# A pool of its own for the small buffers of a float32 decoder block: every large on-chip buffer starts 32 to 192 bytes lower

## The chip, the cores and the metric

The kernel runs on one core of one Trainium2 chip. The time is the device time of one execution in microseconds (us). It was taken three times before the change: 2767.97, 2766.76 and 2764.39 us, median 2766.76 us. A fourth execution, the one that the hardware profiler recorded, took 2759.24 us; its span, from the first to the last instruction, is 2757.5 us, so 1.7 us lie around the span. All durations below come from that execution.

## What is computed

One layer of a decoder for 512 tokens with 2048 channels, all in float32, cut here to what matters:

```python
def mixer(h, pos, w_in, w_a, w_b, w_o):
    proj = h @ w_in
    q_a, k_a, v_a, q_b, k_b, v_b, qi, ki, wi, g_a, g_b = jnp.split(proj, offsets, axis=-1)
    y_a = stick_breaking_attention(q_a, k_a, v_a) @ w_a
    y_b = dsa_attention(rope(q_b), rope(k_b), v_b, rope(qi), rope(ki), wi) @ w_b
    merged = jax.nn.sigmoid(g_a) * y_a + jax.nn.sigmoid(g_b) * y_b
    return merged @ w_o

def conv_ffn(h, w_up, conv_w, conv_b, w_down):
    u = h @ w_up
    u = conv_b + sum(conv_w[i] * shifted(u, i) for i in range(3))
    a, b = jnp.split(u, 2, axis=-1)
    return (jax.nn.silu(a) * b) @ w_down
```

Around both parts stand an RMS norm with a scale and a shift that are computed from a vector c (a 2048 x 12288 matrix times c), and a gated residual add. The products with the large weight matrices are nearly all of the work.

## The kernel before

**Products of three.** Each large product of float32 numbers is made of three matmuls of the type float32r. Every operand is split in two: a high part (a copy to float32r on ScalarE, line 133 for weights, 162 for data) and a low part (the difference, on VectorE, lines 135 and 164). `mm3` (lines 142 to 146) then issues high x high (L143), high x low (L144) and low x high (L145) into one accumulator. Its first argument is the stationary operand of the array, its second the moving one. Weights come by DMA from SyncE's queue into eight buffers `raw` (128 partitions x 4096 bytes), and their two parts lie in three buffers `wh` and three `wl` of the same size. Data live in 62 slots `F` of 128 x 2048 bytes.

**Which operand moves.** A group of rows in the profile names it as `out<-moving,stationary`. In the first stage (the query part of the token indexer, 16 steps of 7 products) the data `F` move, 512 columns wide, past weights in `wh` and `wl`. In the next (the values of the first attention) the weights move and the data stand. Then come the 31 Strassen units of the projection (`unit`, line 199 on), where data halves of 256 columns move past weights. After the two attentions follow w_a and w_b (512 columns, data moving), eight units of w_o, the up-projection (512 wide for its first three pairs of tiles, then units of 256), and the down-projection, where weights move again, 512 wide. In the last part of that, four column blocks for each of four token blocks, both operands lie in slots `F`. The two products with `w_tail` take only 80 columns of weights at a time: step k has its weights 320 x k bytes into the buffer.

**Where buffers lie.** The order of work is the program's, arranged by a scheduler that knows no addresses. A pool lays out its buffers one tag after another, in the order in which tags are first asked for. A buffer takes a multiple of 32 bytes. All buffers were in one pool `sb`, so a small one (`eps`, 4 bytes in each partition, or `c_col`, 64 bytes) shifts all that come after it:

| buffers | first address before | remainder by 128 | remainder by 256 |
|---|---|---|---|
| `F` (62 x 2048 bytes), `raw` (8 x 4096), `T` | 26912, 153888, 22816 | 32 | 32 |
| `wl`, `wh` (3 x 4096 each) | 186720, 199008 | 96 | 96 |
| `w` (2 x 2048) | 211296 | 96 | 96 |
| `sp`, `ta` (2 x 2048 each) | 215456, 219552 | 32 | 160 |
| `soft` (5120) | 223680 | 64 | 192 |

The buffers of one tag follow each other without a gap, so all of a tag have its remainder.

Of the kernel before, what the change touches and what calls it, by code (L numbers as in the profile page):

```python
# [10 lines left out]
F32 = mybir.dt.float32  # L11
# [7 lines left out]
P = 128  # L19
D = 2048  # L20
S = 512
KT = D // P
HD = 128
NH = 8
IDXH = 16
IDXD = 64
TOPK = 128
NQB = S // P
# [48 lines left out]
def block_kernel(ctx: ExitStack, tc: tile.TileContext, A: dict, out: bass.AP):  # L77
    nc = tc.nc
    sb = ctx.enter_context(tc.tile_pool(name="sb", bufs=1))
    pp = ctx.enter_context(tc.tile_pool(name="pp", bufs=1, space=PSUM))  # L80
    dr = ctx.enter_context(tc.tile_pool(name="dr", bufs=1, space=bass.MemoryType.DRAM))

# [2 lines left out]
    def nm(s):  # L85
        counter[0] += 1
        return f"{s}_{counter[0]}"

    def t2k(tag, bufs, dt=F32, w=S):
        return sb.tile([P, w], dt, tag=tag, bufs=bufs, name=nm(tag))  # L90
# [26 lines left out]
    g_mix, g_ffn = (vec[:, 96 + i * KT : 96 + (i + 1) * KT] for i in range(2))  # L117
    mask = sb.tile([P, 2, P], BF16, tag="mask", name="mask")
    cw = sb.tile([P, 2 * NJ, 4], F32, tag="cw", name="cw")
    eps = sb.tile([P, 1], F32, tag="eps", name="eps")  # L120
    nc.vector.memset(eps, EPS)


# [200 lines left out]
        return cb  # L324

    cb = c_spread()
    c_col = sb.tile([P, KT], F32, tag="c_col", name="c_col")
    nc.scalar.dma_start(c_col, A["c_col"])
    act(c_col, c_col, AF.Silu)

# [1 line left out]
    def rms(squares, blocks=range(NQB), bank=outs):  # L332

        total = bank()
        at = slice(blocks[0] * P, (blocks[-1] + 1) * P)
        for b in blocks:
            for i, t in enumerate(squares):
                mm(total[:, b : b + 1], t[:, b * P : (b + 1) * P], ones[:, :1], start=b == blocks[0] and i == 0,
                   stop=i == len(squares) - 1, skip_group_check=True)
        r = sb.tile([P, NQB], F32, tag="r", bufs=2, name=nm("r"))  # L340
        rb = r[:, blocks[0] : blocks[-1] + 1]
        act(rb, total[:, blocks[0] : blocks[-1] + 1], AF.Sqrt, scale=1.0 / D, bias=eps)
        nc.vector.reciprocal(rb, rb)
        wide = t2k("T", 2)
        for b in blocks:
            ts(wide[:, b * P : (b + 1) * P], ident, r[:, b : b + 1], None, ALU.mult)
        yield
        out = bank()
        mm(out[:, at], ones, wide[:, at], start=True, stop=True)
        yield out  # L350
# [138 lines left out]

    def rope_tables():  # L490
        f0, f1, f2, f3, f123, f23, fr = _turn_parts()
        inv = sb.tile([64, 1], F32, tag="inv", name="inv")
        nc.scalar.dma_start(inv, A["inv_freq"])
        pos = t2k("T", 2, I32)[:64]
        nc.scalar.dma_start(pos, A["positions"].to_broadcast([64, S]))
        turn = [t2k("w", 2)[:64] for _ in range(2)]

        def nearest(o, i, step):
            m = 1.5 * 2.0**23 * step
            ts(o, i, m, m, ALU.add, ALU.subtract)  # L500

        for half in range(2):
            at = slice(half * HALF, (half + 1) * HALF)
            q1, q2 = (t[:, at] for t in turn)
            tmp = sb.tile([P, 5 * HALF], F32, tag="soft", name=nm("soft"))[:64]
            ang, a2, a1, a0, rn = (tmp[:, i * HALF : (i + 1) * HALF] for i in range(5))
            nc.vector.tensor_copy(ang, pos[:, at])
            ts(ang, ang, inv, None, ALU.mult)
            nearest(a2, ang, 2.0**20)
            tt(ang, ang, a2, ALU.subtract)  # L510
            yield
            nearest(a1, ang, 2.0**8)
            tt(ang, ang, a1, ALU.subtract)
            nearest(a0, ang, 2.0**-4)
            tt(ang, ang, a0, ALU.subtract)
            small = ang
            ts(small, ang, fr, None, ALU.mult)
            yield
            stt(small, a0, f123, small, ALU.mult, ALU.add)
            stt(small, a1, f23, small, ALU.mult, ALU.add)  # L520
            stt(small, a2, f3, small, ALU.mult, ALU.add)
            ts(q1, a1, f0, None, ALU.mult)
            stt(q1, a2, f1, q1, ALU.mult, ALU.add)
            yield
            nearest(rn, q1, 1.0)
            tt(q1, q1, rn, ALU.subtract)
            ts(q2, a1, f1, None, ALU.mult)
            stt(q2, a2, f2, q2, ALU.mult, ALU.add)
            nearest(rn, q2, 1.0)
            tt(q2, q2, rn, ALU.subtract)  # L530
            yield
            stt(q1, a0, f0, q1, ALU.mult, ALU.add)
            tt(q1, q1, q2, ALU.add)
            nearest(rn, q1, 1.0)
            tt(q1, q1, rn, ALU.subtract)
            tt(q1, q1, small, ALU.add)
            yield
            nearest(rn, q1, 1.0)
            tt(q2, q1, rn, ALU.subtract)
            ts(q1, q2, 0.25, None, ALU.add)  # L540
            nearest(rn, q1, 1.0)
            tt(q1, q1, rn, ALU.subtract)
            yield
        TWO_PI = float(np.nextafter(np.float32(2 * np.pi), np.float32(0)))
        q1, q2 = turn
        for n, step in enumerate((64, 32)):
            o = t2k("raw", 8, w=1024)
            for i in range(P // step):
                at = slice(step * i, step * i + step)
                act(o[at, :S], q1[:step], AF.Sin, scale=TWO_PI)  # L550
                act(o[at, S:], q2[:step], AF.Sin, scale=TWO_PI if i % 2 else -TWO_PI)
                if i % 2:
                    yield
            save(rope_d[n], o)
# [109 lines left out]
    for k in range(0, KT, 2):  # L664
        r = t2k("w", 2)
# [19 lines left out]
    def strips(a, b, c):  # L685

        return [b[:, 3 * P : 4 * P], c[:, : 2 * P], b[:, : 3 * P], a[:, : 4 * P]]
# [7 lines left out]
    def indexer():  # L695
# [6 lines left out]
        for b in range(NQB):  # L702
            nc.tensor.transpose(wps[:, b * IDXH : (b + 1) * IDXH], tail[IDXD:TN, b * P : (b + 1) * P],
                                ident[IDXD:TN, IDXD:TN])
        wi = sb.tile([P, NQB, IDXH], F32, tag="wi", name="wi")
        nc.vector.tensor_copy(wi.rearrange("p b h -> p (b h)"), wps[:, : NQB * IDXH])
        bias.extend(slot()[:, : (b + 1) * P] for b in range(1, NQB))
        yield
# [36 lines left out]
        for b in range(1, NQB):  # L745
            sc = bias[b]
            for i in range(TOPK // 8):
                m8 = sb.tile([P, 8], F32, tag="m8", bufs=2, name=nm("m8"))
                nc.vector.max(out=m8, in_=sc)
                nc.vector.match_replace(out=sc, in_to_replace=m8, in_values=sc, imm_value=TAKEN)  # L750
                if i % 2:
                    yield
            ts(sc, sc, TAKEN, NEG, ALU.not_equal, ALU.mult)
# [5 lines left out]

    vb = [[], []]  # L760
    index = indexer()
    run(index)
    run(index)
# [117 lines left out]
    ya = [split(o) for o in ya]  # L881

    def sparse_1(q, k):
        m = sb.tile([P, NQB], F32, tag="m", bufs=2, name=nm("m"))
        s = sb.tile([P, NQB], F32, tag="s", bufs=2, name=nm("s"))
        soft = sb.tile([P, 10 * P], F32, tag="soft", name=nm("soft"))
        lg = strips(*(acc() for _ in range(3)))
        p = strips(*of_soft(soft))
        for b in (2, 0, 1, 3):
            W = (b + 1) * P  # L890
            mm(lg[b], q[:, b * P : (b + 1) * P], k[:, :W], start=b > 0, stop=True, skip_group_check=True)
        for b in (2, 0, 1, 3):
            nc.vector.tensor_tensor_reduce(out=p[b], in0=lg[b], in1=bias[b], scale=HD**-0.5, scalar=-3.0e38,
                                           op0=ALU.add, op1=ALU.max, accum_out=m[:, b : b + 1])
        last = ts(m, m, -1.0, None, ALU.mult)
        for b in (2, 0, 1, 3):
            act(p[b], p[b], AF.Exp, bias=m[:, b : b + 1], accum_out=s[:, b : b + 1])
        return p, s, last
# [45 lines left out]
    for hd in range(NH):  # L944
        p, s, last = sparse_1(*pairs[hd])
# [68 lines left out]
    def norm_late(c1, c2):  # L1014
# [1 line left out]
        c, sq = (c1, c2), (t2k("ta", 2), t2k("sp", 2))  # L1016
        total, rstd = att(), outs()
        wide = t2k("T", 2)
        r = sb.tile([P, NQB], F32, tag="r", bufs=2, name=nm("r"))

        def add_up(t, blocks, first=False):
            for b in blocks:
# [199 lines left out]
    def bank(b):  # L1222
        return [att() for _ in range(4)] if b % 2 == 0 else [acc() for _ in range(3)] + [outs()]
# [214 lines left out]
        return [fetch(x1t[:, t, b * S : (b + 1) * S]) for b in range(2, 4)]  # L1438

    def finish_tokens(t, xs, s):  # L1440
        r = sb.tile([P, NQB], F32, tag="r", bufs=2, name=nm("r"))
        tt(r[:, :2], s[:, :2], s[:, 2:], ALU.add)
        tt(r[:, 2:3], r[:, :1], r[:, 1:2], ALU.add)
        act(r[:, 3:], r[:, 2:3], AF.Sqrt, scale=1.0 / D, bias=eps)
        nc.vector.reciprocal(r[:, 3:], r[:, 3:])
        for b, x in enumerate(xs):
            if t == NQB - 1 and b < 2:
                act(x, x, AF.Copy, scale=r[:, 3:])
            else:
                stt(x, x, r[:, 3:], g_row[b], ALU.mult, ALU.mult)  # L1450
            nc.sync.dma_start(out[t][:, b * S : (b + 1) * S], x)
# [3 lines left out]
    for t in range(NQB):  # L1455
        ahead = operands(t + 1) if t + 1 < NQB else None
        xs = []
        s = sb.tile([P, NQB], F32, tag="s", bufs=2, name=nm("s"))
        for b in range(4):
            if not ps:  # L1460
                ps = bank(t)
# [126 lines left out]
```

## Time and profile before

| | |
|---|---|
| runs | 2764.39 to 2767.97 us, median 2766.76 us |
| profiled execution | 2759.24 us, its span 2757.5 us |
| ScalarE (ACT) busy | 1450.7 us, 53% of the span |
| GpSimd (POOL) busy | 315.3 us, 11% |
| DMA | 550.08 MB, mean 199 GB/s; 164189 packets |
| float32r weight splits on VectorE, 128x1024 | 758 of 1219 ns each (L135) |
| the same on ScalarE | 758 of 1061 ns each (L133) |

The profile gives each engine's busy time; PE is TensorE, DVE is VectorE. Matmuls overlap in the pipe, so the length of one (some 280 ns for 256 columns) is not the time that it costs: that is the distance from its start to the next one's start. A timeline answer has a row for each instruction: start in us, length in us, engine, line, operation, `out<-in`, shape of the array's use (128*128 is 128 rows by 128 stationary columns), and partitions x moving columns.

### The profile page before, as it was taken

To read this page: it belongs to the slowest core of one execution; us is meant where nothing else is said; L and a number is where in the kernel's file an instruction comes from. 1 tells how busy PE (TensorE), PEld (TensorE's weight loads), DVE (VectorE), ACT (ScalarE), POOL (GpSimd) and SP (SyncE) were. 2 spreads that over 40 slices of the span, in tenths; PEclk is the share of its full clock that TensorE was granted. 3 is DMA by queue.
4 is the path that set the end of the run, shared out by engine and by line. 5 is a ranking of instruction groups with operands and counts; after the bars stand their busy time and mean duration, and the time that the engine had idled before them with its cause. 6 is when DMAs were issued, how large, how long until landed. Compare 5 with 4: busy or idle time off the path is not lost.

```text
span 2757.5 us, 47708 instructions
## 1 busy us (share of the span) xinstructions
PE 2697.6 (98%) x18704; PEld 2457.7 (89%) x18704; DVE 2411.3 (87%) x3452; ACT 1450.7 (53%) x2045; POOL 315.3 (11%) x519
## 2 busy tenths in 40 slices
PE   8999999999999999999999999999999999999997
PEld 6779999999998777879999999999999998887876
DVE  8978979988887899889879999999999997888886
ACT  4444454455556655434557555555555555546452
POOL 0010000000012011111230000000000000002122
PEclk9999999999999999999999999999999999999998
DMA  9973456756567467865783566666666446569786
GB/s 348 354 254 122 156 181 195 232 176 188 166 195 238 133 206 243 279 213 174 233 269 108 179 176 178 187 177 184 176 179 182 130 131 219 151 176 245 193 256 196
DMA packets 164189, 550.08 MB, mean 199 GB/s; under 512 B 21414, under 2 KB 21798, under 8 KB 163964
## 3 DMA queue, kind: packets, MB, share of 16 engines
q1 hardware_dynamic: 116220, 405.34, 45.9%
q0 software_dynamic: 47152, 141.30, 18.4%
q8 instruction: 147, 2.41, 0.4%
q14 instruction: 78, 0.64, 0.1%
q10 hardware_dynamic: 592, 0.39, 0.1%
HBM read 453.71 MB, written 89.83 MB: 197 GB/s over the span
## 4 chain that ended last, share of the span: by engine, by line
PE 67%; DVE 8%; DMA 5%; issue 4%; ACT 1%; POOL 0%; DVEq 0%; POOLq 0%; ACTq 0%; SPq 0%
PE att L145 10%; PE att L143 10%; PE att L144 10%; PE acc L145 10%; PE acc L143 10%; PE acc L144 10%; DVE wl L135 3%; DMA raw<-in_w_x 1%; DMA raw<-in_w_down 1%; PE acc L722 1%; PE acc L816 1%; PE outs L922 1%; DMA raw<-in_w_o 1%; PE outs L145 1%; PE outs L144 1%
## 5 line engine op out<-in xcount | busy, mean ns | idle before, releaser
L133 ACT ACTIVATE wh<-raw 128x1024 fp32r<-128x1024 f32 (+2 forms) x792 | 828.9, 1053 | 962.2 <-DVE raw L237 179.1
L135 DVE TENSOR_TENSOR wl<-raw,wh 128x1024 fp32r<-128x1024 f32 (+2 forms) x792 | 952.6, 1210 | 126.5 <-ACT wh L133 121.8
L143 PE MATMUL acc<-F,wh 128*128 128x256 f32 (+1 forms) x2464 | 709.1, 290 | 12.8 <-ACT wh L133 7.1
L145 PE MATMUL acc<-F,wl 128*128 128x256 f32 (+1 forms) x2464 | 710.6, 289 | 6.1 <-DVE wl L135 6.1
L144 PE MATMUL acc<-F,wh 128*128 128x256 f32 (+1 forms) x2464 | 710.3, 288 | 0.6 <-DVE F L388 0.4
L143 PE MATMUL att<-F,wh 128*128 128x256 f32 (+1 forms) x2448 | 704.8, 289 | 5.8 <-DVE sp L273 4.5
L145 PE MATMUL att<-F,wl 128*128 128x256 f32 (+1 forms) x2448 | 704.2, 288 | 3.3 <-DVE wl L135 3.0
L144 PE MATMUL att<-F,wh 128*128 128x256 f32 (+1 forms) x2448 | 704.5, 288 | 1.2 <-DVE F L164 1.2
L143 PEld LDWEIGHTS acc<-F,wh 128*128 128x128 f32 x2464 | 463.3, 188 | 29.5 <-ACT wh L133 12.2
L145 PEld LDWEIGHTS acc<-F,wl 128*128 128x128 f32 x2464 | 463.0, 188 | 19.2 <-DVE wl L135 8.5
L143 PEld LDWEIGHTS att<-F,wh 128*128 128x128 f32 x2448 | 460.4, 188 | 19.3 <-ACT wh L133 5.2
L144 PEld LDWEIGHTS acc<-F,wh 128*128 128x128 f32 x2464 | 463.8, 188 | 12.9 <-DVE F L388 1.4
L144 PEld LDWEIGHTS att<-F,wh 128*128 128x128 f32 x2448 | 461.3, 188 | 13.6 <-DVE F L164 4.3
L145 PEld LDWEIGHTS att<-F,wl 128*128 128x128 f32 x2448 | 460.3, 188 | 14.3 <-DVE wl L135 5.0
L290 DVE SCALAR_TENSOR_TENSOR raw<-raw,raw 128x1024 f32<-128x1024 f32 x152 | 182.1, 1217 | 0.0
L143 PE MATMUL att<-wh,F 128*128 128x512 f32 x448 | 178.5, 399 | 0.2 <-ACT wh L133 0.2
L145 PE MATMUL att<-wh,F 128*128 128x512 f32 x448 | 176.3, 394 | 0.0
L144 PE MATMUL att<-wl,F 128*128 128x512 f32 x448 | 176.1, 393 | 0.2 <-DVE wl L135 0.2
L233 DVE TENSOR_TENSOR raw<-raw,raw 128x1024 f32<-128x1024 f32 x80 | 97.4, 1218 | 42.3 <-DMA raw<-in_w_x 24.3
L144 PE MATMUL acc<-wl,F 128*128 128x512 f32 x288 | 114.0, 396 | 2.4 <-DVE wl L135 2.4
L145 PE MATMUL acc<-wh,F 128*128 128x512 f32 x288 | 113.7, 395 | 0.0
L143 PE MATMUL acc<-wh,F 128*128 128x512 f32 x288 | 112.2, 392 | 0.0
(364 smaller groups left out, 3621.3 us busy)
## 6 DMA issues: line engine op xcount, KB each, us to landing
raw<-in_w_up SPq DMA_DIRECT2D x164, 512.0 KB, 4.0
raw<-in_w_ada SPq DMA_DIRECT2D x152, 512.0 KB, 5.2
raw<-in_w_x SPq DMA_DIRECT2D x128, 512.0 KB, 4.3
raw<-in_w_down SPq DMA_DIRECT2D x104, 512.0 KB, 5.3
xd<-F POOLq DMA_DIRECT2D x64, 256.0 KB, 2.5
F<-xd POOLq DMA_DIRECT2D x64, 256.0 KB, 4.7
raw<-in_w_o SPq DMA_DIRECT2D x32, 512.0 KB, 5.1
soft<-in_w_gate SPq DMA_DIRECT2D x32, 512.0 KB, 4.1
```

Of the source, the lines that this page charges most:

```text
L133: pins["wh"] = act(wh, raw, AF.Copy)
L135: pins["wl"] = tt(wl, raw, wh.bitcast(F32), ALU.subtract)
L143: mm(ps, ah, bh, start=first, stop=False, skip_group_check=not check)
L144: mm(ps, ah, bl, start=False, stop=False, skip_group_check=not check)
L145: return mm(ps, al, bh, start=False, stop=last, skip_group_check=not check)
L233: last_v = tt(s, a21, a22, ALU.add)
L290: return stt(raw, raw, 1.0, cb[half], ALU.mult, ALU.mult, accum_out=macc[:, t, half : half + 1])
L722: mm(dots[:, :W], both[:, b * P : (b + 1) * P], kiR[i][:, :W], start=i == 0, stop=i == 1)
L816: mm(o, negtri if tri else negones, i, start=False, stop=True, skip_group_check=True)
L922: mm(o[:, b * P : (b + 1) * P], vs[kb][:, hd % 4 * HD : (hd % 4 + 1) * HD], pT[b][:, kb * P : (kb + 1) * P], start=kb == 0, stop=kb == b)
```

## The change

A second pool, `tiny`, is opened right behind `sb`, and the small buffers get their place in it: `eps`, `c_col`, `r`, `inv`, `wi`, `m8`, `m` and `s`. Sizes, counts of buffers and all uses stay.

```diff
     sb = ctx.enter_context(tc.tile_pool(name="sb", bufs=1))
+    tiny = ctx.enter_context(tc.tile_pool(name="tiny", bufs=1))
     pp = ctx.enter_context(tc.tile_pool(name="pp", bufs=1, space=PSUM))
...
-    eps = sb.tile([P, 1], F32, tag="eps", name="eps")
+    eps = tiny.tile([P, 1], F32, tag="eps", name="eps")
...
-    c_col = sb.tile([P, KT], F32, tag="c_col", name="c_col")
+    c_col = tiny.tile([P, KT], F32, tag="c_col", name="c_col")
...
-        r = sb.tile([P, NQB], F32, tag="r", bufs=2, name=nm("r"))
+        r = tiny.tile([P, NQB], F32, tag="r", bufs=2, name=nm("r"))
...
-        inv = sb.tile([64, 1], F32, tag="inv", name="inv")
+        inv = tiny.tile([64, 1], F32, tag="inv", name="inv")
...
-        wi = sb.tile([P, NQB, IDXH], F32, tag="wi", name="wi")
+        wi = tiny.tile([P, NQB, IDXH], F32, tag="wi", name="wi")
...
-                m8 = sb.tile([P, 8], F32, tag="m8", bufs=2, name=nm("m8"))
+                m8 = tiny.tile([P, 8], F32, tag="m8", bufs=2, name=nm("m8"))
...
-        m = sb.tile([P, NQB], F32, tag="m", bufs=2, name=nm("m"))
-        s = sb.tile([P, NQB], F32, tag="s", bufs=2, name=nm("s"))
+        m = tiny.tile([P, NQB], F32, tag="m", bufs=2, name=nm("m"))
+        s = tiny.tile([P, NQB], F32, tag="s", bufs=2, name=nm("s"))
...
```

In the two built programs every engine has the same instructions in the same order, with the same semaphores, waits and shapes, and the same buffer of a tag is given to the same use. The addresses in the accumulators' memory and in device memory are the same too. What differs is the address in on-chip memory:

| buffers | first address after | moved by | remainder by 256 |
|---|---|---|---|
| `F`, `raw`, `T`, `macc`, `mod`, `amp` | 26880, 153856, 22784, 21504, 22272, 22656 | -32 | 0 (`amp` 128) |
| `wl`, `wh`, `w` | 186624, 198912, 211200 | -96 | 0 |
| `sp`, `ta` | 215296, 219392 | -160 | 0 |
| `soft` | 223488 | -192 | 0 |
| `eps`, `c_col`, `r`, `inv` | 228608, 228640, 228704, 228768 | up | 0, 32, 96, 160 |
| `wi`, `m8`, `m`, `s` and all ahead of `eps` | | 0 | as before |

More of the change, by code (lines that the diff above doesn't have):

```diff
@@ L1018, in norm_late @@
         wide = t2k("T", 2)
-        r = sb.tile([P, NQB], F32, tag="r", bufs=2, name=nm("r"))
+        r = tiny.tile([P, NQB], F32, tag="r", bufs=2, name=nm("r"))
         def add_up(t, blocks, first=False):
@@ L1440, in finish_tokens @@
     def finish_tokens(t, xs, s):
-        r = sb.tile([P, NQB], F32, tag="r", bufs=2, name=nm("r"))
+        r = tiny.tile([P, NQB], F32, tag="r", bufs=2, name=nm("r"))
         tt(r[:, :2], s[:, :2], s[:, 2:], ALU.add)
@@ L1457, in block_kernel @@
         xs = []
-        s = sb.tile([P, NQB], F32, tag="s", bufs=2, name=nm("s"))
+        s = tiny.tile([P, NQB], F32, tag="s", bufs=2, name=nm("s"))
         for b in range(4):
```

## The prediction

> **What bounds the kernel now.** I read the page's totals and its chain first, then engine times stage by stage, then start times of matmuls.
>
> ```profile
> span 2757.5 us, 47708 instructions
> ...
> PE 2697.6 (98%) x18704; PEld 2457.7 (89%) x18704; DVE 2411.3 (87%) x3452; ACT 1450.7 (53%) x2045; POOL 315.3 (11%) x519
> ...
> PE 67%; DVE 8%; DMA 5%; issue 4%; ACT 1%; POOL 0%; DVEq 0%; POOLq 0%; ACTq 0%; SPq 0%
> ```
>
> TensorE is busy for 98% of the span and is 67% of the chain that ended last. So a change that moves no instruction can matter mainly by how fast TensorE streams. The stages (length, then busy time and instructions of each engine, granted clock, DMA share, GB/s):
>
> ```profile
> core 0: us, PE busy (x) PEld busy (x) DVE busy (x) ACT busy (x) POOL busy (x), PEclk, DMA share, GB/s
> 0.00:120.00 120.00, 105.17 (x418) 80.88 (x419) 104.71 (x193) 54.53 (x78) 8.20 (x17) 0.99 0.95 346
> 264.00:380.00 116.00, 115.24 (x977) 114.84 (x976) 102.79 (x151) 51.80 (x65) 7.04 (x13) 1.00 0.51 165
> 1200.00:1255.00 55.00, 55.00 (x237) 44.30 (x236) 47.62 (x81) 21.09 (x29) 9.18 (x18) 1.00 0.68 225
> 1600.00:2290.00 690.00, 690.00 (x6055) 686.04 (x6055) 643.30 (x760) 386.32 (x496) 45.31 (x68) 1.00 0.61 169
> 2300.00:2690.00 390.00, 387.18 (x1683) 314.62 (x1682) 320.82 (x395) 201.16 (x262) 59.28 (x80) 1.00 0.72 208
> 2701.00:2729.00 28.00, 28.00 (x125) 23.20 (x124) 16.80 (x31) 8.11 (x21) 10.08 (x19) 1.00 0.82 254
> ```
>
> The first 120 us hang on DMA (share 0.95, TensorE 12% idle). In all the others TensorE never stops for long and the granted clock is 1.00. Yet rows 2 and 4, the same 256-wide matmuls of `unit`, have 8.4 and 8.8 of them per us. The start times say why. First and last of 27 steps each, in both stretches:
>
> ```profile
> 289.73 0.28 PE L145 MATMUL att<-F,wl 128*128 128x256 f32 x1
> ...
> 292.91 0.28 PE L145 MATMUL att<-F,wl 128*128 128x256 f32 x1
> ```
>
> ```profile
> 1689.78 0.28 PE L145 MATMUL att<-F,wl 128*128 128x256 f32 x1
> ...
> 1692.84 0.28 PE L145 MATMUL att<-F,wl 128*128 128x256 f32 x1
> ```
>
> 3.18 us / 27 = 117.8 ns against 3.06 / 27 = 113.3 ns, at full clock, without a wait between. The 512-wide ones, 12 steps each, differ too:
>
> ```profile
> 1239.71 0.39 PE L143 MATMUL acc<-F,wh 128*128 128x512 f32 x1
> ...
> 1242.51 0.39 PE L143 MATMUL acc<-F,wh 128*128 128x512 f32 x1
> ```
>
> ```profile
> 2390.22 0.39 PE L143 MATMUL att<-wh,F 128*128 128x512 f32 x1
> ...
> 2392.97 0.39 PE L143 MATMUL outs<-wh,F 128*128 128x512 f32 x1
> ```
>
> ```profile
> 2709.81 0.39 PE L143 MATMUL acc<-F,F 128*128 128x512 f32 x1
> ...
> 2712.53 0.39 PE L143 MATMUL acc<-F,F 128*128 128x512 f32 x1
> ```
>
> That is 233.3 ns where data move past weights, 229.2 where weights move past data, and 226.7 where both lie in `F`. These three differ in the **distance** from the moving operand's address to the stationary one's, modulo 256: 96 - 32 = 64, 32 - 96 = 192, and 0. The products with `w_tail` test it, as their stationary block moves by 320 bytes (64 modulo 256) every three matmuls. The L143 rows of five steps and the next product's first:
>
> ```profile
> 200.04 0.40 PE L143 MATMUL acc<-F,wh 128*80 128x512 f32 x1
> ...
> 200.75 0.40 PE L143 MATMUL acc<-F,wh 128*80 128x512 f32 x1
> ...
> 201.44 0.39 PE L143 MATMUL acc<-F,wh 128*80 128x512 f32 x1
> ...
> 202.12 0.39 PE L143 MATMUL acc<-F,wh 128*80 128x512 f32 x1
> ...
> 202.80 0.40 PE L143 MATMUL acc<-F,wh 128*80 128x512 f32 x1
> ...
> 203.51 0.39 PE L143 MATMUL acc<-F,wh 128*128 128x512 f32 x1
> ```
>
> Three matmuls take 0.71, 0.69, 0.68, 0.68 and 0.71 us. The stationary block starts at distance 0, 64, 128, 192, 0. Counted to the block's end (320 bytes on, as if the weights were read from the last column) the distance is 64, 128, 192, 0, 64. A full block is 512 bytes, so there start and end agree. Then all match: 64 costs 0.71 (full block 3 x 233.3 = 0.70), 192 costs 0.68 (3 x 229.2 = 0.69), 0 costs 0.68 (3 x 226.7 = 0.68). So I read the excess over 226.7 as a conflict between the weight load, which runs during the matmul before, and the moving stream, set by their distance modulo 256. That the cause is a conflict is inferred; that the cadence differs by place is measured.
>
> The Trainium skill, "TensorE: Matmul & The Clock Gate" (Step-by-step: what each phase is for), says the opposite: two independent read ports, so that loading the next weights "doesn't steal SBUF read bandwidth from the running matmul". By it the distance would not matter, and the sum would be 0; no row above fits that, with 226.7 and 233.3 ns at one clock.
>
> **The change part by part.** It adds, removes and moves no instruction, DMA or wait. After it `F`, `wh` and `wl` all begin at a multiple of 256, so the distance of every full 128-column block is 0. The counts:
>
> ```profile
> L143 PE MATMUL acc<-F,wh 128*128 128x256 f32 x2240 | 623.3, 278 | 3.4 <-DVE sp L273 2.2 <-DVE F L977 0.5 <-ACT wh L133 0.3
> L143 PE MATMUL att<-wh,F 128*128 128x512 f32 x448 | 178.5, 399 | 0.2 <-ACT wh L133 0.2
> L144 PE MATMUL acc<-wl,F 128*128 128x512 f32 x288 | 114.0, 396 | 2.4 <-DVE wl L135 2.4
> L144 PE MATMUL outs<-wl,F 128*128 128x512 f32 x96 | 37.6, 392 | 0.0
> L143 PE MATMUL att<-F,wh 128*128 128x512 f32 x208 | 82.4, 406 | 0.1
> ```
>
> 1. *512 wide, data moving*: six groups of 208 (two banks, three lines) are 1248. 16 x 7 x 3 = 336 of them lie in the first 120 us, where DMA is late, and gain nothing. 912 x (233.3 - 226.7) = 6.0 us.
> 2. *512 wide, weights moving*: 3 x (448 + 288 + 96) = 2496, at 229.2 - 226.7 = 2.5 ns: 6.2 us.
> 3. *256 wide*, at distance 64 now in one of two cadences. The largest slow stretch is the row 264:380; its 977 matmuls would gain 4.5 ns each, 4.4 us. Stretches of 17 to 28 us at 399, 651, 731 and 771 and shorter ones behind 1266 add about 1400 matmuls by the same start times, 6.3 us. At distance 0 no row has a steady 256-wide stream, so this term is bounded: -10.7 us if all run at 113.3, and above zero if the fast ones become slow (the first rival). I take -10.7, because the 512-wide stream at distance 0 (226.7 = 2 x 113.3) is the clean one.
> 4. *Everything else*: a DMA into `soft`, at remainder 192, and one into `raw`, at 32, land alike (rows below, both 512 KB), so I take nothing. The bounds are 0.1 of 4.0 us in the DMA-bound 120 us, 3 us either way. The small buffers' operations keep their shapes; nothing is seen to hang on their places.
>
> ```profile
> raw<-in_w_up SPq DMA_DIRECT2D x164, 512.0 KB, 4.0
> soft<-in_w_gate SPq DMA_DIRECT2D x32, 512.0 KB, 4.1
> ```
>
> The sum is -22.9 us of TensorE streaming. TensorE is busy for nearly all of those stages, but is 67% of the chain; between 0.67 (15 us) and 1 (23 us) I take 0.7: **-16 us**. What is late next is VectorE: in 1600:2290 it is busy 643.3 of 690 us.
>
> 2759.24 - 16 = 2743 us for an execution like the profiled one. The median of the runs stands 7.5 us above that one, so 2766.8 - 16 = **2751 us**.
>
> **The rivals.** Within 0.2%, some 5.5 us, a measurement of this kernel can't tell a change from none.
>
> ```profile
> L722 PE MATMUL acc<-F,F 128*128 128x512 f32 x32 | 10.5, 410 | 0.0
> ...
> L145 PE MATMUL att<-F,F 128*128 128x512 f32 x32 | 12.5, 390 | 0.0
> ...
> L891 PE MATMUL acc<-F,F 128*128 128x512 f32 x16 | 8.2, 592 | 0.0
> ...
> L891 PE MATMUL acc<-F,F 128*128 128x128 f32 x16 | 3.1, 273 | 0.0
> ```
>
> *Slower: the 256-wide stream locks into its slow cadence.* It holds a cadence over many products, with the same remainders, so what it had at the last stall decides too. Short bursts at L722, both operands in `F` at distance 0, take 410 ns where the steady stream takes 390: distance 0 alone is no guarantee. Place: the units. There are 6 x 2240 = 13440 such matmuls, some 11000 of them fast. Price: 4.5 ns each, 50 us for all, less 12 us of terms 1 and 2: up to 2805; for half of them 2780. It decides from (12.2 + 5.5) / 4.5 ns = 3900 matmuls on. Against it: the clean 226.7 at distance 0. Chance 0.23.
>
> *No change.* The distance isn't the cause (the stages differ in other traffic too), or the gain is waited away on VectorE or DMA. Time 2761 to 2772, chance 0.20. The `w_tail` rows speak against the first, the 7% that VectorE has free against the second.
>
> *Much faster: the start itself costs.* A plain float32 pass streams at (592 - 273) / 384 = 0.83 ns per column (L891), and half of that is 0.415; the float32r stream, with twice the bytes per time, has 226.7 / 512 = 0.443 at best, 1/16 more. No float32r operand begins at a multiple of 64 bytes now, so that 1/16 may be the price of the start. If it goes too, 13440 x 7 ns + 3400 x 14 ns = 140 us of streaming go, more than the 7% that VectorE leaves free allows beside its waits: half arrives, with the 16 us some 85: 2680. Against it: remainders 32 and 96 have the same floor. Chance 0.12. The Trainium skill's page on TensorE (Back-to-back issue gap) has 262 and 518 cycles for 256 and 512 columns; at its 2.4 GHz those would be 109 and 216 ns, and the sum by them would be near this rival's. The 113.3 and 226.7 ns of this trace differ from it.
>
> *The change doesn't do what it says*: it does, by the addresses; no chance of its own.
>
> **How the numbers follow.** Forecast 0.45 (2740 to 2760), much faster 0.12, no change 0.20, slower 0.23. Of the range's two ends the low one, 2722, takes in a part of the much faster case (a third of its gain), and the high one, 2795, three quarters of the slower case with the 3 us of DMA; about 0.15 to 0.2 stay out. Faster by over 0.2%: 0.45 + 0.12 = 0.57; within: 0.20; slower: 0.23.
>
> **What would show it.** The steps between L143 rows around 1240 and 2390 at 226.7 ns bear out terms 1 and 2; 233 and 229 ns there would sink them. The counts of matmuls in equal windows of the units (1025 in 116 us when fast) show term 3 or the first rival. Steps below 226 or 113 ns show the third. Group means of DVE and ACT (1219 and 1061 ns for weight splits) should stay within 5 ns. If cadences improve as said and the time doesn't, the loss is in waits on VectorE (`wl`, L135) or DMA.

## The result, and the profile after

The changed kernel took 2810.47 us (median of 4 executions, 2805.64 to 2811.28); the kernel before took 2767.36 us beside it. The ratio of the means is 1.0138, with a 95% interval from 1.0092 to 1.0184: **slower by 1.4%**, where 2751 us had been forecast and 2795 us was the end of the range. The profiled execution took 2810.0 us, 50.8 us more than the one of before (2759.24).

The totals and the chain of waits of the changed kernel:

```profile
span 2808.2 us, 47708 instructions
...
PE 2757.4 (98%) x18704; PEld 2532.8 (90%) x18704; DVE 2419.4 (86%) x3452; ACT 1453.3 (52%) x2045; POOL 314.5 (11%) x519
...
PE 86%; DVE 6%; DMA 3%; issue 3%; ACT 1%; POOL 0%; DVEq 0%; SPq 0%; ACTq 0%; POOLq 0%
```

The same instructions, and TensorE's part of the chain went up from 67% to 86%: the kernel is now bound by TensorE more than before. Engine by stage, columns as in the prediction:

```profile
264.00:380.00 116.00, 115.24 (x959) 114.89 (x958) 100.84 (x146) 50.78 (x65) 7.02 (x13) 1.00 0.49 160
1200.00:1255.00 55.00, 55.00 (x245) 45.53 (x244) 47.36 (x84) 20.89 (x29) 10.64 (x20) 1.00 0.68 228
1600.00:2290.00 690.00, 690.00 (x5723) 686.01 (x5722) 612.41 (x718) 371.36 (x471) 45.77 (x67) 1.00 0.59 162
```

The clock is 1.00 throughout. Row 2 (512 wide) has 245 matmuls in 55 us where 237 stood: faster. Row 3 (256 wide, never idle) has 5723 where 6055 stood: 690 / 5723 = 120.6 ns for each, where it was 114.0. The start times give the steps, first and last of 27 steps at 256 columns and of 12 at 512:

```profile
1689.34 0.28 PE L144 MATMUL acc<-F,wh 128*128 128x256 f32 x1
...
1692.58 0.28 PE L144 MATMUL acc<-F,wh 128*128 128x256 f32 x1
```

```profile
1239.28 0.39 PE L144 MATMUL acc<-F,wh 128*128 128x512 f32 x1
...
1242.00 0.39 PE L144 MATMUL acc<-F,wh 128*128 128x512 f32 x1
```

```profile
2389.22 0.39 PE L145 MATMUL att<-wl,F 128*128 128x512 f32 x1
...
2391.94 0.39 PE L145 MATMUL att<-wl,F 128*128 128x512 f32 x1
```

3.24 us / 27 = **120.0 ns** at 256 columns, a cadence that the kernel before does not have in its units. 2.72 us / 12 = **226.7 ns** at 512 columns, whichever operand moves. The length column still says 0.28 us for the 256-wide ones, as before; only the distance of the starts tells the two kernels apart.

The other engines show no change of speed. The weight splits on VectorE and ScalarE, and two of the loads:

```profile
L136 DVE TENSOR_TENSOR wl<-raw,wh 128x1024 fp32r<-128x1024 f32 x758 | 923.9, 1222 | 136.0 <-ACT wh L134 129.0
L134 ACT ACTIVATE wh<-raw 128x1024 fp32r<-128x1024 f32 x758 | 802.0, 1059 | 998.1 <-PE acc L145 190.1 <-DVE raw L238 175.9 <-PE att L145 162.0
```

```profile
raw<-in_w_up SPq DMA_DIRECT2D x164, 512.0 KB, 3.9
...
soft<-in_w_gate SPq DMA_DIRECT2D x32, 512.0 KB, 4.0
```

1222 and 1059 ns against 1219 and 1061, and loads that land within 0.1 us of before: the new addresses change nothing here that can be seen.

**The account.** Over all start times of the two traces, steps without a stall (below 130 ns at 256 columns, below 245 at 512; the 80-column blocks of `w_tail` and the last steps, L1114 to L1116, included) are:

| steps | before | after | difference |
|---|---|---|---|
| 256 wide, data moving | 13642 at 114.1 ns | 13700 at 120.0 ns | 13642 x 5.9 = +80 us |
| 512 wide, data moving | 1354 at 233.2 ns | 1360 at 227.6 ns | 1354 x -5.6 = -7.6 us |
| 512 wide, weights moving | 2437 at 229.2 ns | 2432 at 227.2 ns | 2437 x -2.0 = -4.9 us |

That is +68 us of streaming, and +50.8 us of time. The other 17 us are stalls that went. The matmuls come in the same order in both traces, so they can be compared one by one: 60 of the 256-wide steps that stalled before run without a stall after (21.6 us became 7.2), and 62 that stall in both took 22.7 us where they had taken 25.1. That is nearly all of the 17 us. The largest named part is a wait for VectorE at L273, the sum into `sp` that reads an accumulator. In TensorE's waits of before it has two rows (us in total, times, longest):

```profile
PE att L143 <- DVE sp L273: 4.5, 6, 2.0
...
PE acc L143 <- DVE sp L273: 2.2, 3, 1.2
```

After the change one such row is left:

```profile
PE acc L144 <- DVE sp L274: 0.8, 1, 0.8
```

A slower TensorE gives VectorE more time: 6.7 us became 0.8 here alone.

### The profile page after: what moved, and what is told of

Read it like the earlier page. It is cut to its first block, busy times and chain, and to the rows that moved or that the text cites. A ratio compares the mean times of both kernels' runs of the same rounds, so it can differ in the third digit from the quotient of the medians.

```text
span 2808.2 us, 47708 instructions
## 1 busy us (share of the span) xinstructions
PE 2757.4 (98%) x18704; PEld 2532.8 (90%) x18704; DVE 2419.4 (86%) x3452; ACT 1453.3 (52%) x2045; POOL 314.5 (11%) x519
## 4 chain that ended last, share of the span: by engine, by line
PE 86%; DVE 6%; DMA 3%; issue 3%; ACT 1%; POOL 0%; DVEq 0%; SPq 0%; ACTq 0%; POOLq 0%
PE att L146 13%; PE att L144 13%; PE att L145 13%; PE acc L145 13%; PE acc L146 13%; PE acc L144 13%; DVE wl L136 1%; DMA raw<-in_w_down 1%; PE acc L723 1%; PE acc L817 1%; PE outs L923 1%; PE outs L146 1%; PE outs L145 1%; PE outs L144 1%; PE acc L892 1%
## 5 line engine op out<-in xcount | busy, mean ns | idle before, releaser
L144 PE MATMUL acc<-F,wh 128*128 128x256 f32 (+1 forms) x2464 | 720.4, 294 | 11.2 <-ACT wh L134 7.3
L146 PE MATMUL acc<-F,wl 128*128 128x256 f32 (+1 forms) x2464 | 722.2, 293 | 3.7 <-DVE wl L136 3.6
L145 PE MATMUL acc<-F,wh 128*128 128x256 f32 (+1 forms) x2464 | 722.2, 293 | 0.7 <-DVE F L389 0.7
L145 PE MATMUL att<-F,wh 128*128 128x256 f32 (+1 forms) x2448 | 716.9, 293 | 1.2 <-DVE F L165 1.2
L146 PE MATMUL att<-F,wl 128*128 128x256 f32 (+1 forms) x2448 | 716.2, 293 | 1.7 <-DVE wl L136 1.7
L144 PE MATMUL att<-F,wh 128*128 128x256 f32 (+1 forms) x2448 | 716.5, 294 | 0.2 <-ACT F L163 0.2
L144 PEld LDWEIGHTS acc<-F,wh 128*128 128x128 f32 x2464 | 471.5, 191 | 25.8 <-ACT wh L134 10.2
L146 PEld LDWEIGHTS acc<-F,wl 128*128 128x128 f32 x2464 | 471.6, 191 | 15.0 <-DVE wl L136 5.6
L145 PEld LDWEIGHTS acc<-F,wh 128*128 128x128 f32 x2464 | 471.9, 192 | 11.8 <-DVE F L389 1.7
L145 PEld LDWEIGHTS att<-F,wh 128*128 128x128 f32 x2448 | 469.5, 192 | 12.5 <-DVE F L165 4.3
L144 PEld LDWEIGHTS att<-F,wh 128*128 128x128 f32 x2448 | 469.4, 192 | 11.4 <-issue 2.0
L146 PEld LDWEIGHTS att<-F,wl 128*128 128x128 f32 x2448 | 469.2, 192 | 10.6 <-DVE wl L136 2.5
```

Source lines behind the costliest of these rows:

```text
L144: mm(ps, ah, bh, start=first, stop=False, skip_group_check=not check)
L145: mm(ps, ah, bl, start=False, stop=False, skip_group_check=not check)
L146: return mm(ps, al, bh, start=False, stop=last, skip_group_check=not check)
```

## The experiments

Three theories stood after the result. **D**: the distance between the stationary and the moving operand, modulo 256 bytes, sets the cadence, and at distance 0 it is bad for 256 columns though good for 512. **S**: the start of `F` at a multiple of 256 is what costs. **O**: other engines' traffic, on buffers that now all begin alike, gets in TensorE's way. All kernels below are the changed kernel with buffers shifted and every instruction in its place, except `bench` and `bench2`, which are bursts of matmuls alone.

### One part undone: c_col, or eps

`d64` puts only `c_col` back, which moves `wl` and `wh` on by 64:

```diff
-    c_col = tiny.tile([P, KT], F32, tag="c_col", name="c_col")
+    c_col = sb.tile([P, KT], F32, tag="c_col", name="c_col")
```

> Only c_col goes back among the big buffers: F, raw, T stay at remainder 0, wl and wh begin at 64 (modulo 256). Theory D (the distance between the stationary and the moving operand modulo 256 sets the cadence; here 64 again, as before the change): 256-wide units at 113.3 or 117.8 ns as before, none at 120; 512-wide with data moving 233.3 ns, with weights moving 229.0 ns; time about 2767 us. Theory S (it is the start of F, or of the moving operand, at a multiple of 256 that costs): units stay at 120.0 ns, time about 2810 us. Theory O (traffic of other engines on buffers that now all begin alike): raw and F stay alike, so units at 120 still or nearly, about 2800 us or more.

2778.87 us (2762.80 to 2792.59 in ten executions), ratio to before 1.0016 (0.9979 to 1.0054). In its profiled execution, first and last of 27 steps in the units and of 12 at 512 columns:

```profile
1687.99 0.28 PE L144 MATMUL att<-F,wh 128*128 128x256 f32 x1
...
1691.17 0.28 PE L144 MATMUL att<-F,wh 128*128 128x256 f32 x1
```

```profile
1238.76 0.39 PE L146 MATMUL acc<-F,wl 128*128 128x512 f32 x1
...
1241.56 0.39 PE L146 MATMUL acc<-F,wl 128*128 128x512 f32 x1
```

117.8 and 233.3 ns: 120.0 is gone and 233.3 is back, though `F` and `raw` still begin at 0. That is against S and O.

`d0_f32` puts only `eps` back, at the front, which moves all big buffers on by 32 and keeps the distance 0:

```diff
-    eps = tiny.tile([P, 1], F32, tag="eps", name="eps")
+    eps = sb.tile([P, 1], F32, tag="eps", name="eps")
```

> Only eps goes back to the front: every big buffer is 32 bytes further on, F, raw, wl and wh all begin at remainder 32 and the distance stays 0. Theory D: nothing changes against the changed kernel, units at 120.0 ns, all 512-wide at 226.7 ns, about 2810 us. Theory S: units at 113.3 (and perhaps 117.8) ns, with 226.7 ns for the 512-wide, about 2745 to 2765 us. Theory O: all buffers still begin alike, 120.0 ns, about 2810 us.

2810.22 us (2807.82 to 2812.85), ratio 1.0145 (1.0101 to 1.0189), and again in the units:

```profile
1688.07 0.28 PE L146 MATMUL acc<-F,wl 128*128 128x256 f32 x1
...
1691.31 0.28 PE L146 MATMUL acc<-F,wl 128*128 128x256 f32 x1
```

120.0 ns with no float32r operand at a multiple of 64. S falls: not where a buffer begins counts, but how far the two operands are apart. So of the eight small buffers that went to the second pool, one, `c_col`, made the difference: it stood between `F` and the weights.

### The other distances

A pad of 32 to 96 bytes, `c_col`, `inv` (32) or `amp` (128) between `raw` and `wl` give six more distances. The edit for 128:

```diff
     cb = c_spread()
-    c_col = tiny.tile([P, KT], F32, tag="c_col", name="c_col")
+    sb.tile([P, 16], F32, tag="pad", name="pad")
+    c_col = sb.tile([P, KT], F32, tag="c_col", name="c_col")
```

> wl and wh begin at 128, F at 0: distance 128 in both directions. Theory D: a cadence of its own class; from the w_tail rows of the kernel before (0.690 us for three) 230 ns for every 512-wide matmul; for 256-wide no row shows it, anything from 113.3 to 120 ns, the same in every unit. Time from 2760 (113.3 ns) to 2815 us (120 ns). Theory S: units at 120.0 ns and 512-wide at 226.7 ns, about 2810 us.

> wl and wh begin at 192, F at 0: distance 192 with data moving, 64 with weights moving, the mirror of the kernel before. Theory D: the two 512-wide classes change places: data moving 229.0 ns, weights moving 233.3 ns; the 256-wide units (distance 192) in a class that no row shows yet, between 113.3 and 120 ns. Time from 2755 (113.3 ns) to 2815 us (120 ns). Theory S: 120.0 and 226.7 ns, about 2810 us.

> F at remainder 0, wl and wh at 32: distance 32 (224 with weights moving). Half steps between the four distances run so far. Theory I (the cost goes over evenly from one distance to the next): 512-wide with data moving about 230 ns (between 226.7 and 233.3), weights moving about 228; 256-wide units about 118 ns on the mean (between 120.0 at distance 0 and 114 to 116 at distance 64); about 2790 us. Theory K (only the distance in whole steps of 64 bytes counts): one of its neighbours exactly, so units at 120.0 ns with 226.7 ns and 2810 us, or units at 113.3 / 117.8 ns with 233.3 ns and 2757 to 2795 us.

> F at remainder 0, wl and wh at 96: distance 96 (160 with weights moving). Theory I: 512-wide about 233 ns with data moving, 231 with weights moving; units about 117 ns (between 114 to 116 at distance 64 and 118.7 at 128); about 2795 us. Theory K: the cadences of distance 64 (2757 to 2795 us) or those of 128 (2811 us).

> F at remainder 128, wl and wh at 32: distance 160 (96 with weights moving). Theory I: 512-wide about 231 ns with data moving, 233 with weights moving; units about 118 ns (between 118.7 at 128 and 117.2 at 192); about 2803 us. Theory K: the cadences of 128 (2811 us) or of 192 (2795 us).

> F at remainder 128, wl and wh at 96: distance 224 (32 with weights moving). Theory I: 512-wide about 228 ns with data moving, 230 with weights moving; units about 118.6 ns (between 117.2 at 192 and 120.0 at 0); about 2803 us. Theory K: the cadences of 192 (2795 us) or of 0 (2810 us).

Mean steps of each profiled execution, and the executions. With weights moving the distance is the negative one:

| distance of `wl`, `wh` from `F` | 256 wide | 512, data moving | 512, weights moving | time, us |
|---|---|---|---|---|
| 0 (the changed kernel) | 120.0 | 227.6 | 227.2 | 2805.64 to 2811.28 |
| 32 | 118.3 | 233.2 | 233.3 | 2807.02 to 2813.83 |
| 64 (`d64`) | 116.1, of 113.3 and 117.8 | 233.2 | 229.1 | 2762.80 to 2792.59 |
| 96 | 118.0 | 234.0 | 233.3 | 2805.08 to 2808.04 |
| 128 | 118.7 | 232.5 | 232.7 | 2809.49 to 2811.88 |
| 160 | 120.0 | 233.3 | 234.2 | 2830.04 to 2834.87 |
| 192 | 117.2 | 230.0 | 233.3 | 2791.13 to 2800.07 |
| 224 | 116.9 | 233.1 | 233.3 | 2788.64 to 2797.76 |

Distances 64 and 192 change places with the direction, as D says. The half steps fit neither of their theories: 32 has 233 ns at 512 columns, not 230, and is none of its neighbours, nor is 96 or 224. Single numbers do fit: 118.3 ns at 32, and the time at 224, which is that of 192. At 128, 512 columns take some 232.6 ns, where the `w_tail` rows had promised 230. Each multiple of 32 is a class of its own, and the row for 160 is the worst: its units are as slow as at 0, and its 512-wide matmuls pay too. At 512 columns 0 is best, as forecast. At 256 columns 0 is the worst, with 160, and 64 is the best, which is where the kernel before had been by the size of `c_col`.

### The cadence by itself

`bench` has no kernel around it: one matmul burst after another.

```python
for s in range(steps):
    q = s % 8
    ...
    mm(o, ah, bh, start=s == 0, stop=False, skip_group_check=True)
    mm(o, ah, bl, start=False, stop=False, skip_group_check=True)
    mm(o, al, bh, start=False, stop=s == steps - 1, skip_group_check=True)
nc.vector.tensor_copy(keep[:k, :n], o)
```

> A kernel of its own that computes nothing of the reference: one load, then bursts of 48 back-to-back float32r matmuls in the order of the units (three products for each block of weights, 16 blocks), each burst with its own width and distance, no DMA and nothing on VectorE or ScalarE during a burst. Theory D (distance alone, a conflict inside TensorE's reads): the cadences of the kernels show here too: 512-wide 226.7 / 233.3 / 232.5 / 229 ns at distances 0 / 64 / 128 / 192, 256-wide 120.0 / 113.3 or 117.8 / 118.7 / 117.2 ns. With 96, 64 and 32 stationary columns at distance 0, 256 wide: if the conflict is with the weight load, the 6.7 ns above 113.3 shrink with the columns loaded (about 5, 3.3, 1.7 ns); if the moving stream alone pays, they stay 6.7 ns. Theory O (traffic of other engines): 113.3 and 226.7 ns at every distance here. The bursts at distance 64 show how often each lock is taken.

At a granted clock of 1.00, and without the very first burst, which has stalls in it, the distances repeat: 256 wide 119.9, 118.3, 113.3 or 117.8, 117.3, 118.7 to 120.0, 120.1, 117.8 and 116.8 ns at 0, 32 and so on to 224; 512 wide 227, 233.3, 233.3, 234.2, 232.3, 233.3, 228.9 and 233.3 ns. Nothing below 226.7 or 113.3 turned up, in steps of 16 either. O falls, since the cadences need no other engine. Two bursts at distance 64, one right behind the other, with nothing between them but a copy out of the accumulator, first and last of 27 steps of each:

```profile
98.63 0.28 PE L116 MATMUL acc<-M,W 128*128 128x256 f32 x1
...
101.81 0.28 PE L116 MATMUL acc<-M,W 128*128 128x256 f32 x1
...
105.03 0.28 PE L116 MATMUL acc<-M,W 128*128 128x256 f32 x1
...
108.09 0.28 PE L116 MATMUL acc<-M,W 128*128 128x256 f32 x1
```

117.8 ns, then 113.3. Of 13 such bursts 3 were slow. Of ten that followed six 512-wide matmuls without a pause none was.

With 64 stationary columns instead of 128 (the weight load reads half as much), at distance 0 and then at 64:

```profile
934.95 0.28 PE L117 MATMUL acc<-M,W 128*64 128x256 f32 x1
...
938.01 0.28 PE L117 MATMUL acc<-M,W 128*64 128x256 f32 x1
...
947.36 0.28 PE L117 MATMUL acc<-M,W 128*64 128x256 f32 x1
...
950.58 0.28 PE L117 MATMUL acc<-M,W 128*64 128x256 f32 x1
```

113.3 ns at distance 0, where 128 columns take 120.0, and 119 ns at 64, where they take 113.3 or 117.8. So the number of stationary columns takes part, which a moving stream that pays alone could not explain. The rows of the output shrink with them and no burst separates the two, so that it is the weight load is a reading and not shown. The expected shrinking (5, 3.3, 1.7 ns) did not come either: 96, 64 and 32 columns at distance 0 gave 2.6, 0 and 4.5 ns above 113.3. It is not a toll for each column loaded; perhaps load and stream meet or miss each other in a pattern, which is not shown.

bf16 operands, at distance 0:

```profile
1586.72 0.27 PE L115 MATMUL acc<-MB,WB 128*128 128x256 bf16 x1
...
1589.67 0.27 PE L115 MATMUL acc<-MB,WB 128*128 128x256 bf16 x1
```

109.3 ns, and 215.8 ns at 512 columns, the same to 0.1 ns at 0, 64, 128 and 192. The Trainium skill, "TensorE: Matmul & The Clock Gate" (Back-to-back issue gap), has 262 and 518 cycles in its table of the isolated gap, which at its 2.4 GHz are 109.2 and 215.8 ns. For bf16 these runs agree with it, and with the two independent read ports of the page's section "Step-by-step: what each phase is for". For float32r they don't: 113.3 and 226.7 ns at best, and a distance that matters.

### Two distances at once, and a kernel that beats both

`bench2` gives `wh` and `wl` distances of their own.

> A kernel of its own that computes nothing of the reference: bursts of float32r matmuls with wh and wl at distances of their own, all 64 pairs of multiples of 32. For each pair six bursts of 36 matmuls 256 wide, and one burst of 24 each 512 wide with data moving and with weights moving. If the cadence depends on distance alone, the pairs with equal distances repeat the values of the first such kernel (256-wide 120.0 at 0, 113.3 or 117.8 at 64, 117 to 120 elsewhere), and the pair 64 with 192 is the only other one near 113.3 ns (113.4 and 113.8 ns there). A pair at 113.3 ns in all six bursts, with 512-wide not above 233 ns, would make a kernel of some 2750 us in every execution; if there is none, no placement at multiples of 32 bytes of these two tiles beats distance 64.

First and last of 27 steps, both at distance 0, and then the pair 64 (`wh`) and 192 (`wl`):

```profile
40.17 0.28 PE L113 MATMUL acc<-M,W 128*128 128x256 f32 x1
...
43.41 0.28 PE L113 MATMUL acc<-M,W 128*128 128x256 f32 x1
...
990.60 0.28 PE L113 MATMUL acc<-M,W 128*128 128x256 f32 x1
...
993.66 0.28 PE L113 MATMUL acc<-M,W 128*128 128x256 f32 x1
```

120.0 and 113.3 ns. The pair stays at 113.3 to 113.5 in six bursts of six; 64 with 64 has two at 117.8, and in every other of the 64 pairs half of the bursts or more stand above 115 ns. The 512-wide ones of the pair take, behind their first eight steps, 231.7 (data moving) and 229.7 ns (weights moving). So it was built:

```diff
-    amp = sb.tile([P, 2, KT], F32, tag="amp", name="amp")
...
     cb = c_spread()
-    c_col = tiny.tile([P, KT], F32, tag="c_col", name="c_col")
+    sb.tile([P, 24], F32, tag="pad", name="pad")
+    inv = sb.tile([64, 1], F32, tag="inv", name="inv")
+    c_col = sb.tile([P, KT], F32, tag="c_col", name="c_col")
...
         if not k:
+            amp = sb.tile([P, 2, KT], F32, tag="amp", name="amp")
             total = next_x()
...
-        inv = tiny.tile([64, 1], F32, tag="inv", name="inv")
```

> The changed kernel with wh at distance 64 and wl at distance 192 from F (amp, inv, c_col and a pad are put between raw, wl and wh; no instruction changes its place). The bursts of this pair ran at 113.3 ns in six of six, 231.7 ns (512 wide, data moving) and 229.7 ns (weights moving). If the distances alone decide in the kernel as in the bursts: every stretch of the units at 113.3 ns, no 117.8 ns and no 120.0 ns, 512-wide near 231.7 and 229.7 ns, and about 2750 us in every execution, against 2756 to 2798 us of the kernel before and 2810 of the changed one. If stalls of the kernel can lock this pair into a slow cadence too, the units show stretches above 116 ns and the executions spread as before, about 2757 to 2800 us.

2753.49 us (2751.44 to 2755.74), ratio to before **0.9938 (0.9915 to 0.9961)**, in its totals and in the units:

```profile
span 2749.6 us, 47708 instructions
...
PE 2688.8 (98%) x18704; PEld 2448.4 (89%) x18704; DVE 2408.6 (88%) x3452; ACT 1450.1 (53%) x2045; POOL 314.3 (11%) x519
```

```profile
1688.05 0.28 PE L145 MATMUL acc<-F,wh 128*128 128x256 f32 x1
...
1691.11 0.28 PE L145 MATMUL acc<-F,wh 128*128 128x256 f32 x1
```

113.3 ns here, and 113.5 on the mean of all 13648 steps. Apart from the first seven or so steps behind a stall, means of eight steps above 116 ns are found only between stalls near 1430 us, in runs of at most 17 steps. The 512-wide steps have means of 231.8 and 230.5 ns. It beats both kernels, and its executions lie within 4.3 us of each other.

## Why the prediction was wrong

**What bounds the kernel** was right: TensorE's streaming, and a change of addresses alone moved the time by it. The distance modulo 256 as the cause was right too; `d64` and `d0_f32` show it, and the bursts repeat it.

**Terms 1 and 2** (512 wide) were forecast at -6.0 and -6.2 us and came out at -7.6 and -4.9; 1.8 of the 7.6 us lie in the first 120 us, which term 1 had left out. 226.7 ns at distance 0 held in 222 of 272 stretches of twelve steps; nearly all the others are the first behind a stall or a change of width.

**Term 3 is the step that failed**: "I take -10.7, because the 512-wide stream at distance 0 (226.7 = 2 x 113.3) is the clean one". It carried what 512 columns do over to 256. The runs show +80 us in its place: at distance 0 the 256-wide stream runs at 120.0 ns, in the kernel and by itself, and no fast cadence turned up: all 482 stretches of 27 steps in the changed kernel's units lie between 119.4 and 120.0 ns. The rows at hand that were nearest spoke against the clean reading and were put aside. They are the short bursts at L722 with both operands in `F`, which the prediction read by the lengths of the records, 410 ns for 390; lengths do not show the cadence, start times do. The first burst of the kernel before, eight matmuls merged into one row:

```profile
877.37 1.45 PE L722 MATMUL acc<-F,F 128*128 128x256 f32 x8
```

Its first two are 256 wide, and the trace has the first three starts at 877.37, 877.49 and 877.61 us: 118 and 120 ns, at distance 0. Of the 32 such matmuls at L722, 19 run without a stall, with steps of 118.3 ns on the mean. Bursts so short do not prove a steady cadence, but they were the only 256-wide float32r rows at distance 0, and they were not at 113.3 ns.

**The first rival** had the place right (the units) and the sign. Its price was too low: it took 117.8 ns, the slowest cadence that the trace had shown for units, as the worst. 120.0 is 6.7 ns above 113.3, not 4.5, so its 2805 us and the range's 2795 us were short. That 2805 still came near is partly luck: it let all of the streaming arrive in the time, where three quarters did. The bound for an operation in a place that no row shows was drawn from rows in another place.

**The share that arrives**, 0.7 of the streaming, came close, 50.8 of 68 us being 0.75, but by luck: it was worked out for a gain, of which new waits would eat a part. Here a loss was softened by stalls that went.

**Much faster**, the 1/16 as the price of the start, falls: 226.7 ns stays where every operand begins at a multiple of 256 and where none does. **Term 4**, nothing for DMA, VectorE and ScalarE, held.

**Open** is whether it is the weight load that disturbs the stream, and why at some distances; it would need a matmul stream with no weight loads, which was not tried. So is what decides at a stall which cadence is taken at distance 64.

## What to carry to other kernels

Before a buffer is aligned or moved, read the starts of back-to-back matmuls, width by width, and the operands' addresses modulo 256: a small buffer can hold a good distance by accident, and what is best for one width need not be for another. Where no row shows a width at the new distance, measure it with a burst, or bound it from both sides of what is known; a clean value at another width bounds nothing. Where an unexplained cadence comes and goes between executions, two operands at distances of their own may be steadier than one distance for both.

## What the runs showed of the hardware that was not expected

The float32r stream has more than one stable cadence at the same addresses, and in this trace it changes only at a stall: in the kernel before, each of the 68 unbroken runs of 20 or more 256-wide steps keeps, behind its first few steps, either 113.3 or 117.8 ns to its end. Units at distance 64, ahead of and behind a wait for VectorE (27 steps in the first pair, 24 in the second):

```profile
724.65 0.28 PE L145 MATMUL att<-F,wl 128*128 128x256 f32 x1
...
727.71 0.28 PE L145 MATMUL att<-F,wl 128*128 128x256 f32 x1
730.01 0.35 PE L143 MATMUL att<-F,wh 128*128 128x256 f32 x1 [2.03 <-DVE sp L273]
...
730.32 0.28 PE L145 MATMUL att<-F,wl 128*128 128x256 f32 x1
...
733.15 0.28 PE L145 MATMUL acc<-F,wl 128*128 128x256 f32 x1
```

3.06 us / 27 = 113.3 ns, a stall of 2 us, then 2.83 / 24 = 117.9. The spread of that kernel goes with it: beside the first experiments its 16 executions took 2756.75 to 2795.35 us, and none on record took more than 2798.36, less than every execution of the changed kernel. `d64`, with the same distances, took 2783.55 us in the profiled execution with 116.1 ns on the mean, 24.3 us more than the profiled one of before with 114.1: 13642 x 2.0 ns = 27 us. The kernels at other distances, and the pair of 64 and 192, spread by 2 to 9 us.

Even at its best float32r is slower than bf16 in the same bursts: 113.3 against 109.3 ns at 256 columns, 226.7 against 215.8 ns at 512.
